# Hand-ordered slices of a decoder trunk: chunks that add first, activations one row tile per piece, their sample part on GpSimd, later x transposes and tables

## The chip, the cores and the metric

The kernel runs on one core of one Trainium2 chip. The metric is the device time of one execution in microseconds (us), as the median of several runs. A core has a matrix engine (TensorE, PE in the profile, with its weight loads as PEld), three engines for elementwise work (VectorE or DVE, ScalarE or ACT, GpSimd or POOL), and queues through which transfers (DMA) are issued; here SyncE (SP) issues the loads of weights and GpSimd the smaller transfers. Each engine works through its own list of instructions in order, and waits at an instruction until what it needs is there.

## The reference, cut to what matters

One layer of a trunk is computed for 256 prompt tokens and for 8 sequences of 8 sample tokens, 320 columns together, in float32. A conditioning vector per sequence gives six rows of modulation; the first two scale and shift the normed input `h`, which then meets one wide weight matrix `w_in`.

```python
mod = jax.nn.silu(c) @ w_ada + b_ada
sh1, sc1, g1, sh2, sc2, g2 = [m[:, None, :] for m in jnp.split(mod, 6, axis=-1)]
h = _rmsnorm(x, norm1_g) * (1 + sc1) + sh1
p = h @ w_in
sizes = [D_QK, D_QK, D_V, D_V, D_POOL, D_MODEL, D_MODEL]
q, k, v, og, u, ga, gb, alr = jnp.split(p, idx, axis=-1)
...
merged = jax.nn.sigmoid(ga) * y_a + jax.nn.sigmoid(gb) * y_b
x = x + g1 * (merged @ w_o)
...
x = x + g2 * ((jax.nn.silu(gate) * up) @ w_down)
```

The prompt has one conditioning vector, each sample sequence has its own. So the modulation of a tile of `h` is one instruction with per-row scalars for the 256 prompt columns, and two instructions (multiply, add) with broadcast operands for the 64 sample columns.

## The kernel before

Activations lie transposed: 16 row tiles `k` of 128 model channels by 320 tokens. Every float32 product is made of three: weights and activations are split into a high part (`whi`, `hh`: a cast on ScalarE, L152 and L293) and a low part (`wlo`, `hl`: a subtraction on VectorE, L153 and L294), and `mm3` (L166 to L168) adds high by high, high by low and low by high in PSUM.

The first head cannot wait until all of `sh1` and `sc1` are known, since `w_ada` is large. So its products with `w_in` are cut along the contracted dimension into slices of row tiles 0-1, 2-3, 4-7 and 8-15 (`SLICES`). For a slice, each of eleven units of 256 output columns (q, k, u, two each of v, og, ga and gb) is worked in pieces of two row tiles; a piece is 12 matmuls. The first three slices are 11, 11 and 22 pieces, 44 in all, and are written out by hand: inside `manual_schedule` each engine takes the instructions in the order of the code. What follows `manual.close()`, the fourth slice first, is ordered by a scheduler.

A unit's partial sum goes from PSUM to SBUF at the end of each slice (`evac`): in the first slice it is copied, by ScalarE for the first unit of a kind and by VectorE for the second; in later slices VectorE adds it (L347, 128x640). PSUM holds two such partial sums (`pmain`, two buffers), so the third unit waits for the evacuation of the first.

Around the pieces stands a plan. Before piece `p` is multiplied, the weights of piece `p + 3` are split (`cut`). The weights of `w_in` arrive in three buffers `raw`, those of `w_ada` in ten buffers `araw`, both on SP's queue, in order: an issue that waits for a free buffer holds up those behind it. After the pieces in `BURST_AT` comes a burst: 32 products (64 in the first two bursts) of the conditioning with `w_ada` on TensorE (L427). When a group of row tiles has all its bursts, it is closed (`close`): a copy on ScalarE, a transpose on TensorE and three small VectorE instructions give `mod`. Groups are row tiles 2-3, 4-7, 8-11 and 12-15, and they close after the bursts at pieces 6, 18, 30 and 41. `x_tr` transposes `x` for a tile (L130, then a copy, L492), `x_norm` multiplies by the reciprocal norm (on GpSimd, L497) and, from tile 8 on, spills the transposed `x` to DRAM from GpSimd's queue (L499). `x_mod` then modulates and splits the tile:

```python
def x_mod(k):
    affine(xhs[k], 1, 0, k)
    hilo(hh[k], hl[k], xhs[k])
```

`affine` is three VectorE instructions (L298 for the prompt columns, L299 and L300 for the sample columns), `hilo` the cast on ScalarE (L293) and the subtraction on VectorE (L294). All tiles of a group are modulated at once, after its close. `tables` issues four transfers from GpSimd's queue (the gate projection's weights `walr`, the constants `cum`, `cst` and the masks); `cum` is cast by VectorE at L595, `walr` is used by `alr_proj` between the second and third unit of the fourth slice. `spills` issues eight more spills from GpSimd's queue after the last of tile 15 (L631), and one small copy (L632). Each transfer of GpSimd's queue waits until the transfer eight before it has landed.

Of the kernel before, what the change touches and what calls it, by code (L numbers as in the profile page):

```python
# [11 lines left out]
F32 = mybir.dt.float32  # L12
# [3 lines left out]
ALU = mybir.AluOpType  # L16
# [4 lines left out]
P = 128  # L21
TP, NB, LS = 256, 8, 8
TS = NB * LS
T = TP + TS
# [15 lines left out]
BURST_AT = (3, 6, 9, 12, 15, 18, 21, 24, 27, 30, 33, 35, 38, 41)  # L40
# [43 lines left out]
def body(tc, A):  # L84
# [198 lines left out]
    def mods(sec, kt):  # L283
        return mod[:, sec * KT + kt, 1:9].unsqueeze(2).broadcast_to([P, NB, LS])

    def s3(ap):
        return ap.rearrange("p (b t) -> p b t", t=LS)
# [4 lines left out]
    def hilo(hi, lo, x):  # L292
        S.copy(hi, x)  # L293
        V.tensor_sub(lo, x, hi.bitcast(F32))  # L294

    def affine(x, a, b, kt):

        V.tensor_scalar(x[:, 0:TP], x[:, 0:TP], modp(a, kt), modp(b, kt), op0=ALU.mult, op1=ALU.add)  # L298
        V.tensor_tensor(s3(x[:, TP:T]), s3(x[:, TP:T]), mods(a, kt), op=ALU.mult)  # L299
        V.tensor_tensor(s3(x[:, TP:T]), s3(x[:, TP:T]), mods(b, kt), op=ALU.add)  # L300

    xspill = dp.tile([KT, P, T], F32, name="xspill")
    mix = ExitStack()
# [71 lines left out]
    with tc.tile_pool(name="head", bufs=1) as xp:  # L375
# [92 lines left out]
        for i in (0, 2, 1):  # L468
            n = P if i < 2 else TS
# [28 lines left out]
            if k >= 8:  # L498
                spilled[:] = [nc.gpsimd.dma_start(xspill[k], xTs[k]).ins]  # L499

        def x_mod(k):

            affine(xhs[k], 1, 0, k)
            hilo(hh[k], hl[k], xhs[k])

        us = units(0)
        us = [u for u in us if u[0] in "qku"] + [u for u in us if u[0] not in "qku"]
        chunks, pieces, begins = [], [], []
        for k0, k1 in SLICES[:-1]:
            begins.append(len(pieces))  # L510
            for u in us[:3]:
                for k in range(k0, k1, 2):
                    pieces.append((u, k, len(chunks), k - k0, 0, k == k0, k + 2 == k1))
                chunks.append((u[2], k0, k1 - k0, 2 * P))
            for n in range(3, len(us), 2):
                for k in range(k0, k1, 2):
                    for j in range(2):
                        pieces.append((us[n + j], k, len(chunks), 0, 2 * P * j, k == k0, k + 2 == k1))
                    chunks.append((us[n][2], k, 2, 4 * P))
        begins.append(len(pieces))  # L520
        raws, cuts = [], {}

        def fetch():
# [61 lines left out]
        first.burst(2)  # L585
        first.close()
        cut(0)
        x_mod(0)
        x_mod(1)
        cut(1)  # L590
        cut(2)
        load()
# [34 lines left out]
        def spills():  # L627

            with tc.issue_after(spilled[0]):
                for k in spill:  # L630
                    nc.gpsimd.dma_start(xspill[k], xTs[k])  # L631
                nc.gpsimd.dma_start(A["o_ps"][0, :, 0:PB - LS, :], A["state_pool"][0, :, LS:PB, :])  # L632
# [3 lines left out]
        def at(p, *fs):  # L636
            plan.setdefault(p, []).extend(fs)
# [3 lines left out]
        for n, p in enumerate(BURST_AT):  # L641
            a = bursts[n]
            at(p, lambda a=a: a.burst(2))
            at(p + 1, load)
            at(p + 2, load)
            if n + 1 == len(bursts) or bursts[n + 1] is not a:
                at(p + 1, a.close)
                for i in range(a.nb):
                    k = a.b0 + i
                    q = BURST_AT[n - a.nb + 1 + i // 2]  # L650
                    at(q, lambda k=k: (x_tr(k), x_norm(k)))
                    at(p + 1, lambda k=k: x_mod(k))
                if a.b0 == 8:
                    at(p + 1, tables)
        for p in range(len(pieces)):
            cut(p + 3)
            mul(p)
            for f in plan.pop(p, ()):
                f()
        assert not plan or min(plan) >= len(pieces)  # L660
        manual.close()
        spills()
        us = [u for u in us if u[0] in "qku" or u[1] == 0]
        k0, k1 = SLICES[-1]
# [680 lines left out]
```

## Time and profile before

| what | us |
|---|---|
| median of 3 runs | 1965.68 |
| lowest, highest | 1963.19, 1965.73 |
| the profiled execution, its own time | 1965.06 |
| its span | 1963.3 |
| TensorE busy in the span | 1921.2 (98%) |
| VectorE, ScalarE, GpSimd busy | 998.9, 820.1, 209.1 |
| mean granted TensorE clock | 0.993 of full |

Times in the views are us from the start of the span. "Busy" on TensorE counts a matmul from its start to its modelled end, and matmuls overlap; how fast it really goes is read from the starts of successive matmuls. A row of the timeline has the start, the duration, the engine, the line, the operation, the tiles out<-in, the shape, and in brackets how long the engine had been idle and what it waited for. The granted clock (PEclk) is given per stretch, 1.00 being full speed. The hand-ordered slices run from about 28 us to about 157 us of the span.

### The profile page before, as it was taken

The page shows a single profiled execution, that of the slowest core. Times are in us where ns is not written, and L with a number is a line of the kernel's source. Part 1 is how long each engine was busy: PE and PEld are TensorE (multiplying, and loading weights), DVE is VectorE, ACT ScalarE, POOL GpSimd, SP SyncE. Part 2 cuts the span into 40 slices and gives each one's busy share as a digit, 9 for nine tenths or more (in the row PEclk, how much of TensorE's full clock was granted, in tenths as well). Part 3 has the DMA queues.
Part 4 walks back from the last instruction along what each step waited for, and adds up shares of the span by engine and source line. Part 5 has one row for each costly group of instructions (what it writes and reads, how often), then busy time and mean ns, then how long its engine had stood idle before and what let it go on. Part 6 is the DMA issues. An engine that isn't in the chain of part 4 may idle for free.

```text
span 1963.3 us, 35017 instructions
## 1 busy us (share of the span) xinstructions
PE 1921.2 (98%) x13990; PEld 1823.2 (93%) x13990; DVE 998.9 (51%) x1853; ACT 820.1 (42%) x1465; POOL 209.1 (11%) x362
## 2 busy tenths in 40 slices
PE   6999999999999999999999999999999999999998
PEld 5778988988899889988999999999999999999998
DVE  3654655656356535665574444444444444444554
ACT  4323553643336433643454333433333434344444
POOL 1132202221121112110030000000000000000000
PEclk9999999999999999999999999999999999999999
DMA  9995558758865787369936554444445444444443
GB/s 331 335 359 195 175 170 287 253 186 302 282 228 163 276 301 255 126 237 330 336 128 204 187 190 140 151 151 145 156 142 159 150 151 150 149 147 146 142 150 106
DMA packets 298179, 400.95 MB, mean 204 GB/s; under 512 B 13104, under 2 KB 249536, under 8 KB 297688
## 3 DMA queue, kind: packets, MB, share of 16 engines
q1 hardware_dynamic: 270336, 301.05, 47.2%
q0 software_dynamic: 27680, 97.67, 13.5%
q8 instruction: 109, 1.79, 0.4%
q14 instruction: 54, 0.44, 0.1%
HBM read 374.23 MB, written 24.67 MB: 203 GB/s over the span
## 4 chain that ended last, share of the span: by engine, by line
PE 82%; DMA 2%; issue 1%; DVE 1%; ACT 1%; POOL 0%; ACTq 0%; POOLq 0%; DVEq 0%
PE ps L168 25%; PE ps L166 25%; PE ps L167 25%; PE pm L256 3%; DMA o_gs<-S 1%; PE pm L130 1%; PE pm L908 1%; PE pm L929 1%; PE pm L873 1%; DMA araw<-w_ada 0%; PE pm L862 0%; DVE wlo L153 0%; DMA o_gp<-sf 0%; PE psy L166 0%; PE pm L884 0%
## 5 line engine op out<-in xcount | busy, mean ns | idle before, releaser
L153 DVE TENSOR_TENSOR wlo<-raw,whi 128x512 fp32r<-128x512 f32 x941 | 651.3, 695 | 791.1 <-ACT whi L152 779.4
L152 ACT CAST whi<-raw 128x512 fp32r<-128x512 f32 x941 | 580.7, 621 | 922.5 <-PE ps L167 832.7
L166 PE MATMUL ps<-hh,whi 128*128 128x320 f32 x1408 | 445.4, 316 | 11.6 <-DVE mg L347 3.8
L168 PE MATMUL ps<-hh,wlo 128*128 128x320 f32 x1408 | 440.0, 314 | 1.5 <-DVE wlo L153 1.5
L167 PE MATMUL ps<-hl,whi 128*128 128x320 f32 x1408 | 440.4, 313 | 0.6 <-DVE hl L294 0.4
L166 PE MATMUL ps<-h2h,whi 128*128 128x320 f32 x1408 | 434.5, 309 | 0.0
L167 PE MATMUL ps<-h2l,whi 128*128 128x320 f32 x1408 | 434.2, 309 | 0.0
L168 PE MATMUL ps<-h2h,wlo 128*128 128x320 f32 x1408 | 434.1, 309 | 0.0
L166 PEld LDWEIGHTS ps<-hh,whi 128*128 128x128 f32 x1408 | 268.1, 190 | 28.7 <-issue 11.8
L168 PEld LDWEIGHTS ps<-hh,wlo 128*128 128x128 f32 x1408 | 267.1, 190 | 12.2 <-issue 7.4
L167 PEld LDWEIGHTS ps<-hl,whi 128*128 128x128 f32 x1408 | 267.9, 190 | 5.1 <-issue 2.4
L166 PEld LDWEIGHTS ps<-h2h,whi 128*128 128x128 f32 x1408 | 264.4, 188 | 1.6 <-ACT ah L293 1.2
L168 PEld LDWEIGHTS ps<-h2h,wlo 128*128 128x128 f32 x1408 | 264.4, 188 | 0.2 <-DVE wlo L153 0.2
L167 PEld LDWEIGHTS ps<-h2l,whi 128*128 128x128 f32 x1408 | 264.5, 188 | 0.0
L167 PE MATMUL ps<-al,whi 128*128 128x320 f32 (+1 forms) x668 | 206.3, 309 | 0.0
L168 PE MATMUL ps<-ah,wlo 128*128 128x320 f32 (+1 forms) x668 | 205.7, 308 | 0.0
L166 PE MATMUL ps<-ah,whi 128*128 128x320 f32 (+1 forms) x668 | 205.7, 308 | 0.0
L167 PEld LDWEIGHTS ps<-al,whi 128*128 128x128 f32 x668 | 125.2, 187 | 0.1
L168 PEld LDWEIGHTS ps<-ah,wlo 128*128 128x128 f32 x668 | 125.2, 187 | 0.0
L166 PEld LDWEIGHTS ps<-ah,whi 128*128 128x128 f32 x668 | 125.2, 187 | 0.0
L166 PE MATMUL ps<-mh,whi 128*128 128x320 f32 x256 | 79.4, 310 | 0.8 <-DVE mg L1035 0.8
L167 PE MATMUL ps<-ml,whi 128*128 128x320 f32 x256 | 79.4, 310 | 0.0
(327 smaller groups left out, 1644.8 us busy)
## 6 DMA issues: line engine op xcount, KB each, us to landing
raw<-w_gu SPq DMA_DIRECT2D x176, 512.0 KB, 3.5
raw<-w_in SPq DMA_DIRECT2D x173, 512.0 KB, 4.1
araw<-w_ada POOLq DMA_DIRECT2D x54, 1024.0 KB, 8.0
raw<-w_down SPq DMA_DIRECT2D x80, 512.0 KB, 3.4
raw<-w_ada SPq DMA_DIRECT2D x64, 512.0 KB, 9.9
S<-state_gla POOLq DMA_DIRECT2D x16, 1024.0 KB, 8.5
o_gs<-S POOLq DMA_DIRECT2D x16, 1024.0 KB, 5.8
raw<-w_o SPq DMA_DIRECT2D x32, 512.0 KB, 5.8
```

Source lines behind the costliest of these rows:

```text
L130: PE.transpose(out, in_, ident[:k, :k])
L152: S.copy(hi, raw)
L153: V.tensor_sub(lo, raw, hi.bitcast(F32))
L166: PE.matmul(ps, lhsT=whi, rhs=xhi, start=start, stop=False)
L167: PE.matmul(ps, lhsT=whi, rhs=xlo, start=False, stop=False)
L168: last_mm[:] = [PE.matmul(ps, lhsT=wlo, rhs=xhi, start=False, stop=stop).ins]
L256: last_ada[:] = [PE.matmul(ps[32 * j:32 * j + 32, 0:2 * P], lhsT=scT[:, k0 + r, :], rhs=ada_raw[n][:, r, 2 * j * P:(2 * j + 2) * P], start ...
L873: PE.matmul(pt, lhsT=E["kdn"][:, s, d * P:(d + 1) * P], rhs=E["vn"][:, s], start=s == 0, stop=s == 1)
L908: PE.matmul(pt[32 * j:32 * j + 32, :], lhsT=qeP[:, d, 4 * gg + j, :], rhs=E["S0", gg, d][:, j], start=False, stop=d == 0, tile_position=(0 ...
L929: PE.matmul(pt, lhsT=E["kpn"][:, j, d * P:(d + 1) * P], rhs=E["vp"][:, gg], start=True, stop=True)
```

## The change

It does six things, all in the first head's slices.

- In each of the first three slices the units v, og, ga and gb (chunks of 512 columns, two pieces to a chunk of two row tiles) come before q, k and u (chunks of 256 columns).
- The modulation of a tile is cut in two. `x_hi` holds `affine` and the cast, `x_lo` the subtraction. After a close the tiles of the group are taken one per piece: tile `i` of a group that closes at piece `p + 1` has its `x_hi` at `p + 1 + i` and its `x_lo` at `p + 2 + i`.
- From tile 2 on the two sample instructions of `affine` go to GpSimd.
- The transposes, norms and spills of tiles 12 to 15 move from the bursts at pieces 33 and 35 to those at 38 and 41.
- `tables` moves from after the close of tiles 8-11 to the burst at piece 38.
- Entries of the plan beyond the last piece (here those of tiles 13 to 15) are issued after `manual.close()`, where the scheduler orders them.

```diff
-    def affine(x, a, b, kt):
+    def affine(x, a, b, kt, eng):
         V.tensor_scalar(x[:, 0:TP], x[:, 0:TP], modp(a, kt), modp(b, kt), op0=ALU.mult, op1=ALU.add)
-        V.tensor_tensor(s3(x[:, TP:T]), s3(x[:, TP:T]), mods(a, kt), op=ALU.mult)
-        V.tensor_tensor(s3(x[:, TP:T]), s3(x[:, TP:T]), mods(b, kt), op=ALU.add)
+        eng.tensor_tensor(s3(x[:, TP:T]), s3(x[:, TP:T]), mods(a, kt), op=ALU.mult)
+        eng.tensor_tensor(s3(x[:, TP:T]), s3(x[:, TP:T]), mods(b, kt), op=ALU.add)
...
-        def x_mod(k):
-            affine(xhs[k], 1, 0, k)
-            hilo(hh[k], hl[k], xhs[k])
+        def x_hi(k):
+            affine(xhs[k], 1, 0, k, V if k < 2 else G)
+            S.copy(hh[k], xhs[k])
+        def x_lo(k):
+            V.tensor_sub(hl[k], xhs[k], hh[k].bitcast(F32))
...
         for k0, k1 in SLICES[:-1]:
-            begins.append(len(pieces))
-            for u in us[:3]:
-                for k in range(k0, k1, 2):
-                    pieces.append((u, k, len(chunks), k - k0, 0, k == k0, k + 2 == k1))
-                chunks.append((u[2], k0, k1 - k0, 2 * P))
             for n in range(3, len(us), 2):
                 for k in range(k0, k1, 2):
                     for j in range(2):
                         pieces.append((us[n + j], k, len(chunks), 0, 2 * P * j, k == k0, k + 2 == k1))
                     chunks.append((us[n][2], k, 2, 4 * P))
-        begins.append(len(pieces))
+            for u in us[:3]:
+                for k in range(k0, k1, 2):
+                    pieces.append((u, k, len(chunks), k - k0, 0, k == k0, k + 2 == k1))
+                chunks.append((u[2], k0, k1 - k0, 2 * P))
...
-        x_mod(0)
-        x_mod(1)
+        x_hi(0)
+        x_hi(1)
+        x_lo(0)
+        x_lo(1)
...
-                    q = BURST_AT[n - a.nb + 1 + i // 2]
+                    q = BURST_AT[n - a.nb + 1 + i // 2] if k < 12 else BURST_AT[n - 1 + i // 2]
                     at(q, lambda k=k: (x_tr(k), x_norm(k)))
-                    at(p + 1, lambda k=k: x_mod(k))
-                if a.b0 == 8:
-                    at(p + 1, tables)
+                    at(p + 2 + i, lambda k=k: x_lo(k))
+                    at(p + 1 + i, lambda k=k: x_hi(k))
+                if a.b0 == 12:
+                    at(BURST_AT[n - 1], tables)
...
-        assert not plan or min(plan) >= len(pieces)
         manual.close()
+        for p in sorted(plan):
+            for f in plan[p]:
+                f()
         spills()
```

Three places in the order of the instructions. The first is VectorE's list where the second slice ends and tiles 4 to 7 are modulated. Before, the last of the four tiles and what follows it (`xh_785` is tile 7, `mg_121` a half of gb):

```order
L298 TENSOR_SCALAR xh_785<-xh_785,mod 128x256
L299 TENSOR_TENSOR xh_785<-xh_785,mod 128x64
L300 TENSOR_TENSOR xh_785<-xh_785,mod 128x64
L294 TENSOR_TENSOR hl_108<-xh_785,hh_92 128x320
L153 TENSOR_TENSOR wlo_1002<-raw_815,whi_1001 128x512
L347 SCALAR_TENSOR_TENSOR mg_121<-ps_1007,mg_121 128x640
L153 TENSOR_TENSOR wlo_1026<-raw_873,whi_1025 128x512
L347 SCALAR_TENSOR_TENSOR mg_121<-ps_1029,mg_121 128x640
```

Now (`xh_678` is tile 4, `xh_685` tile 5):

```order
L298 TENSOR_SCALAR xh_678<-xh_678,mod 128x256
L153 TENSOR_TENSOR wlo_984<-raw_869,whi_983 128x512
L347 SCALAR_TENSOR_TENSOR k_336<-ps_989,k_336 128x640
L508 TENSOR_TENSOR hl_105<-xh_678,hh_89 128x320
L298 TENSOR_SCALAR xh_685<-xh_685,mod 128x256
L153 TENSOR_TENSOR wlo_1013<-raw_893,whi_1012 128x512
L334 TENSOR_TENSOR u_338<-ps_1016,u_338 128x2x256
```

Sixteen instructions of four tiles stood in a row between two splits of weights; now a tile has two, and a split and an evacuation stand between them. The second place is GpSimd's list around the tables. Before (`xT_1447`, `xT_1456` are tiles 12 and 13):

```order
L622 DMA walr<-w_in 128x16x16
L623 DMA cum<-cf 128x800
L624 DMA cst<-cf 128x67
L625 DMA msk<-ci 128x256
L497 TENSOR_TENSOR xh_1449<-xT_1447,rx 128x320
L499 DMA xspill<-xT_1447 128x320
L497 TENSOR_TENSOR xh_1458<-xT_1456,rx 128x320
```

Now, right behind the spills of tiles 12 and 13 (`xT_1659`, `xT_1668` are tiles 14 and 15, `xh_1574` is tile 12):

```order
L626 DMA walr<-w_in 128x16x16
L627 DMA cum<-cf 128x800
L628 DMA cst<-cf 128x67
L629 DMA msk<-ci 128x256
L497 TENSOR_TENSOR xh_1661<-xT_1659,rx 128x320
L499 DMA xspill<-xT_1659 128x320
L497 TENSOR_TENSOR xh_1670<-xT_1668,rx 128x320
L499 DMA xspill<-xT_1668 128x320
L635 DMA xspill<-mg_122 128x320 x4
L635 DMA xspill<-mg_124 128x320 x4
L636 DMA o_ps<-state_pool 8x7168
L299 TENSOR_TENSOR xh_1574<-xh_1574,mod 128x64
```

The tables stand between tiles 13 and 14 instead of ahead of 12, and the sample instructions of tiles 12 to 15 come after all spills and the small copy. The third place is VectorE's list at the start of the fourth slice, now (left out is one more addition to `mod`):

```order
L599 CAST cumr<-cum 128x800
L153 TENSOR_TENSOR wlo_1775<-raw_1772,whi_1774 128x512
L447 TENSOR_TENSOR mod<-pm_1686,bada 128x36
L449 TENSOR_TENSOR mod<-mod,vec 128x36
...
L298 TENSOR_SCALAR xh_1574<-xh_1574,mod 128x256
L298 TENSOR_SCALAR xh_1661<-xh_1661,mod 128x256
L298 TENSOR_SCALAR xh_1670<-xh_1670,mod 128x256
L334 TENSOR_TENSOR u_338<-ps_1673,u_338 128x2x256
L153 TENSOR_TENSOR wlo_1791<-raw_1772,whi_1790 128x512
L336 TENSOR_TENSOR u_338<-ps_1673,u_338 128x8x8 x2
L153 TENSOR_TENSOR wlo_1811<-raw_1808,whi_1810 128x512
```

The cast of `cum` stood among the third slice's splits before, 38 rows ahead of the last group's first `mod`; now it stands two rows ahead of it. On TensorE the products of q with tiles 12 to 15 now come behind those of k with tiles 8 to 11 (24 matmuls): after `hh_96` (tile 11) stood `hh_97`, now stands

```order
L166 MATMUL ps_1737<-hh_96,whi_1756 128x320
L167 MATMUL ps_1737<-hl_112,whi_1756 128x320
L168 MATMUL ps_1737<-hh_96,wlo_1757 128x320
L166 MATMUL ps_1807<-hh_93,whi_1810 128x320
L167 MATMUL ps_1807<-hl_109,whi_1810 128x320
L168 MATMUL ps_1807<-hh_93,wlo_1811 128x320
```

with `ps_1737` the sum of q, `ps_1807` that of k. Behind the gate projection the order is the same as before on every engine.

More of the change, by code (lines that the diff above doesn't have):

```diff
@@ L499, in x_norm @@
                 spilled[:] = [nc.gpsimd.dma_start(xspill[k], xTs[k]).ins]
-        def x_mod(k):
-            affine(xhs[k], 1, 0, k)
-            hilo(hh[k], hl[k], xhs[k])
+        def x_hi(k):
[3 more added lines that the diff above has]
+            V.tensor_sub(hl[k], xhs[k], hh[k].bitcast(F32))
         us = units(0)
         us = [u for u in us if u[0] in "qku"] + [u for u in us if u[0] not in "qku"]
-        chunks, pieces, begins = [], [], []
+        chunks, pieces = [], []
         for k0, k1 in SLICES[:-1]:
-            begins.append(len(pieces))
-            for u in us[:3]:
-                for k in range(k0, k1, 2):
-                    pieces.append((u, k, len(chunks), k - k0, 0, k == k0, k + 2 == k1))
-                chunks.append((u[2], k0, k1 - k0, 2 * P))
             for n in range(3, len(us), 2):
```

## The prediction

> **What bounds the kernel now.** I read the page's busy times first, then TensorE's waits, then its timeline around each wait.
>
> ```profile
> PE 1921.2 (98%) x13990; PEld 1823.2 (93%) x13990; DVE 998.9 (51%) x1853; ACT 820.1 (42%) x1465; POOL 209.1 (11%) x362
> PE ps L166 <- DVE mg L347: 3.8, 1, 3.8
> PE pm L427 <- DMA raw<-w_ada: 3.8, 5, 1.3
> PE ps L166 <- ACT hh L293: 3.4, 3, 2.4
> PE ps L166 <- ACT q L349: 1.4, 1, 1.4
> PE pm L130 <- ACT adasb L433: 1.1, 2, 0.8
> ```
>
> The matrix engine is busy for 98% of the span, and the change touches none of its work. So all it can move is TensorE's own waiting in the slices, 13.5 us in these rows, and the slow clock behind it. A wait's row has the total, the number, the longest. The largest, 3.8 us, is at the hand-over from the second slice to the third:
>
> ```profile
> 88.27 0.88 PE L130 MATMUL pm<-cst,xn 128*128 128x128 f32 x6
> 92.98 0.60 PE L166 MATMUL ps<-hh,whi 128*128 128x320 f32 x1 [3.84 <-DVE mg L347]
> 93.39 0.47 PE L167 MATMUL ps<-hl,whi 128*128 128x320 f32 x1
> 98.72 0.46 PE L166 MATMUL ps<-hh,whi 128*128 128x320 f32 x1
> 84.13 0.41 DVE L298 TENSOR_SCALAR xh<-xh,mod 128x256 f32<-128x256 f32 x1
> 90.89 0.49 DVE L294 TENSOR_TENSOR hl<-xh,hh 128x320 fp32r<-128x320 f32 x1 [0.58 <-ACT hh L293]
> 91.41 0.69 DVE L153 TENSOR_TENSOR wlo<-raw,whi 128x512 fp32r<-128x512 f32 x1
> 92.02 0.82 DVE L347 SCALAR_TENSOR_TENSOR mg<-ps,mg 128x640 f32<-128x640 f32 x1
> ```
>
> From 84.13 to 91.4 VectorE does nothing but modulate four tiles, idling at each for ScalarE's cast; splits and evacuations stand behind, and TensorE has no free PSUM. After the wait successive matmuls start 0.267 us apart (20 steps from 93.39 to 98.72), against 0.147 at full clock (38 steps between these rows):
>
> ```profile
> 156.23 0.31 PE L166 MATMUL ps<-hh,whi 128*128 128x320 f32 x1
> 161.81 0.31 PE L168 MATMUL ps<-hh,wlo 128*128 128x320 f32 x1
> SPq L144 <- DVE wlo L153: 58.8, 22, 8.9
> 84.00:88.00 4.00, 4.00 (x49) 3.15 (x48) 2.66 (x10) 0.92 (x2) 0.00 (x0) 1.00 1.06 374
> 88.00:92.00 4.00, 1.15 (x14) 0.64 (x6) 2.74 (x9) 2.06 (x5) 0.00 (x0) 1.00 0.63 228
> 92.00:96.00 4.00, 3.02 (x11) 3.05 (x12) 3.23 (x5) 1.06 (x3) 2.82 (x4) 0.53 0.70 212
> 128.00:132.00 4.00, 3.42 (x28) 2.45 (x30) 3.19 (x5) 3.09 (x7) 2.12 (x3) 1.00 0.41 119
> ```
>
> The same block holds up the loads: SP waited up to 8.9 us for a split to free a weight buffer, with loads of w_ada queued behind. The last four rows end in clock, DMA share and GB/s: 374 GB/s, then 228 and 212 behind the modulation of tiles 4-7, and 119 behind that of tiles 8-11.
>
> **The change, part by part.**
>
> *Tiles one per piece.* At the second slice's end VectorE now has, per piece of 12 x 0.147 = 1.76 us, a split 0.69, an evacuation 0.82, and 0.41 + 0.49 of modulation: 2.4 us. That is more than a piece, but the sample part has left, five such pieces contain a burst and transposes, and no evacuation falls in the third slice's first two pieces. So the wait of 3.84 goes and with it 20 x 0.12 = 2.4 of slow clock: **6.2 us**. The wait at tiles 8 to 11 (next row) gives **0.4**.
>
> ```profile
> 128.93 0.41 PE L166 MATMUL ps<-hh,whi 128*128 128x320 f32 x1 [0.41 <-ACT whi L152]
> L299 DVE TENSOR_TENSOR xh<-xh,mod 128x64 f32<-128x64 f32 x11 | 2.4, 218 | 0.0
> L497 POOL TENSOR_TENSOR xh<-xT,rx 128x320 f32<-128x320 f32 x8 | 7.2, 898 | 58.1 <-ACT xT L492 58.0
> 92.35 0.86 POOL L497 TENSOR_TENSOR xh<-xT,rx 128x320 f32<-128x320 f32 x1 [23.62 <-ACT xT L492]
> 92.75 1.00 DVE L153 TENSOR_TENSOR wlo<-raw,whi 128x512 fp32r<-128x512 f32 x1
> ```
>
> *Sample part on GpSimd.* The trace has no 128x64 product there. Its cost lies between VectorE's 0.22 and GpSimd's 0.90 for five times the columns; I take 0.3. Tile 7's two stand behind two norms and two spills of tiles 8 and 9, which come with the burst just before the third slice, so tile 7 arrives late there: **-0.5** (0 to -1). All others have pieces to spare, except tiles 12 to 15, below. In the last two rows a split that overlaps a GpSimd product takes 1.00 instead of 0.69. By the Trainium skill (SBUF — State Buffer, Who interferes with whom) a VectorE instruction with two SBUF inputs and a GpSimd instruction that reads SBUF lock each other out for a whole instruction. This pair agrees in kind. By the rule the 28 products moved could hold VectorE for 28 x 0.3 = 8 us, an estimate; VectorE has that to spare between hand-overs, so the sum would lose about 1 us at most.
>
> *First pieces.* Both `x_lo` now stand behind both tiles' `affine`, which holds the second matmul by about 0.25; the first chunk is 512 KB instead of 256. Together **-0.4** (0 to -0.9).
>
> *Chunk order.*
>
> ```profile
> 36.44 0.41 PE L166 MATMUL ps<-hh,whi 128*128 128x320 f32 x1 [1.42 <-ACT q L349]
> 35.16 0.62 ACT L152 CAST whi<-raw 128x512 fp32r<-128x512 f32 x1 [3.74 <-DMA raw<-w_in]
> ```
>
> The fourth chunk was needed by the fourth piece, and ScalarE waited 3.74 us for it with q's evacuation behind. Three 512-KB chunks now cover six pieces before a fourth is needed: **+1.4**.
>
> *Loads of w_ada.* In the stretch from 28 to 153 the bursts idled 2.8 us for them:
>
> ```profile
> L427 PE MATMUL pm<-raw,scT 128*32 128x256 f32 (+1 forms) x512 | 28.5, 356 | 2.8 <-DMA raw<-w_ada 2.8
> ```
>
> TensorE comes to the last bursts 6.2 + 0.4 + 1.4 - 0.9 = 7.1 us sooner. The loads do too: against 374 GB/s the three low rows above lost 4 us x (146 + 162 + 255) / 374 = 6.0 us of transfer, and the eight late spills of 160 KB (1.3 MB, 3.4 us) now come behind the last burst. I take **+2.5** (0 to 2.8).
>
> *Entry of the fourth slice.* Before:
>
> ```profile
> 155.70 0.40 PE L166 MATMUL ps<-hh,whi 128*128 128x320 f32 x1
> 176.45 0.31 PE L607 MATMUL pm<-hh,wal 128*128 128x320 f32 x1
> 107.00 1.19 POOL L622 DMA_DIRECT2D walr<-w_in  x1
> L499 POOL DMA_DIRECT2D xspill<-xT x8 | 4.7, 587 | 0.0
> cum<-cf POOLq DMA_DIRECT2D x1, 400.0 KB, 8.8
> 117.30 0.57 DVE L595 CAST cumr<-cum 128x800 fp32r<-128x800 f32 x1
> 124.01 1.93 PE L427 MATMUL pm<-raw,scT 128*32 128x256 f32 x32
> ```
>
> 108 matmuls (15.9 us at full clock) took 20.75; with adasb's wait of 0.8 the loss is 5.7 us. Now a new wait stands there: VectorE's cast of `cum` is ahead of the last `mod`, of u's evacuation and of the low parts for k. From the end of the burst at piece 38, GpSimd does two norms, two spill issues and walr's (0.7 for transpose and copy, then 0.9 + 0.6 + 0.9 + 0.6 + 1.2), so `cum` is issued at +4.9 and lands 8.8 later by its row, at +13.7. The last burst ends at +8.1 (transposes 0.9, three pieces 5.3, burst 1.9). So `cum` lands 5.6 after it; I take X = 5, since the w_ada loads have ended by then. The nearest bound below, half that flight, is X = 1. VectorE then needs the cast 0.57, split 0.69, `mod` 0.57, three L298 1.23, u's 0.69 and 0.35, a split 0.69: k's PSUM is free at X + 4.8. TensorE wants it after transposes 0.9, 48 matmuls 7.05 and the close 0.3, at 8.25: stall X - 3.45 = 1.55, and 0.4 more for k's first low part. The last cast ahead of `hh` of tile 12 (0.62) waits for a buffer that k's matmuls free, then come `hh` 0.46 and `hl` 0.49: 1.75. GpSimd's late sample part has by then had some 14 us and lies beside this. Together 3.7 idle, and slow clock after it, 13 x 0.12 = 1.6: 5.3 against 5.7, **+0.4**. With X = 1 it is 1.75 (+4.0); with X = 5.6 and two slow stretches 7.5 (-1.8).
>
> ```profile
> 240.64 0.41 PE L166 MATMUL ps<-hh,whi 128*128 128x320 f32 x1 [1.29 <-ACT whi L152]
> 242.31 0.59 PE L168 MATMUL ps<-hh,wlo 128*128 128x320 f32 x1 [0.82 <-DVE wlo L153]
> 240.00:244.00 4.00, 2.54 (x10) 2.28 (x11) 3.38 (x4) 2.88 (x6) 1.55 (x1) 0.80 0.00 0
> ```
>
> That short idling slows the clock is read here: two waits of 2.1 us together, and the granted clock is 0.80. By the Trainium skill (TensorE: Matmul & The Clock Gate, Part 1) the clock falls after an idle window of about 3.4 us; by that the entry would cost 3.7 instead of 5.3, and the sum would gain 1.6. This row differs, and I keep to the row.
>
> **Sum:** 6.2 + 0.4 - 0.5 - 0.4 + 1.4 + 2.5 + 0.4 = 10.0 us. Behind the gate projection the order is unchanged, so the block only shifts. Against the profiled execution's 1965.06 that is 1955.1; the median of the runs shown is 0.6 above that execution: **1955.5**. All terms at their low ends give 6.2 + 0.4 - 1 - 0.9 + 1.4 + 0 - 1.8 = 4.3 (1961.4), at their high ends 14.8 (1950.9).
>
> **Rivals.**
>
> (a) *The loads become the bound.* For: DMA shares at the ceiling in most stretches, and 2.8 us of waits already. Against: the 6.0 us recovered. If the loads come only 3.6 us sooner where TensorE comes 7.1, 3.5 us of burst waits are added and the 2.5 is lost: gain 4, 1961.5.
>
> (b) *Everything hidden.* `cum` lands early (8.8 us was under full load), and the entry costs 1.75: gain 14 to 15, 1951.
>
> (c) *Slower: VectorE stuck at the cast of `cum`.* Place: the entry; price: one us per us of X beyond 3.45. For: `walr`, small pieces, is ahead in the queue. Against: 8.4 to 8.8 us was measured with the load at its ceiling. The 9.6 us of the other terms are eaten when X - 3.45 + 5.35 - 5.7 = 9.6, at X = 13.4, a landing twice as slow; at X = 20 the time is 1972.
>
> (d) *The hand-over stays.* GpSimd's list holds tile 7, or 2.4 us of VectorE work per piece does not fit, and half of the 6.2 returns: 1959.
>
> **Chances.** Forecast 0.58 (own range 1952 to 1958.5), (a) 0.14, (b) 0.12, (c) 0.04, (d) 0.12. The range 1950.5 to 1961.5 takes in the low and high ends. A difference of 0.2%, 3.9 us, is what a measurement of this kernel can tell: the forecast, (b), (d) and half of (a) are faster by more, 0.87 with a little kept back; same 0.09; slower 0.04.
>
> **What would show it.** No wait near 89 and a granted clock of 1.00 there; no wait for q near 36; DMA near 375 GB/s through 88 to 132; bursts idling under 1 us; VectorE idle before the cast of `cum` with DMA as releaser, and TensorE waiting for u's evacuation right after; the fourth slice entered some 9 us sooner. A gain below 4 us, or waits of several us at new places among the pieces, would make this wrong.

## The result, and the profile after

| | before | changed |
|---|---|---|
| median of 6 runs each, us | 1963.19 | 1951.28 |
| lowest to highest | 1962.89 to 1965.73 | 1948.69 to 1956.34 |
| ratio, 95% interval | | 0.994, 0.9928 to 0.9951 |
| profiled execution: its own time, span | 1965.06, 1963.3 | 1948.69, 1946.9 |

The change saves 11.9 us by the medians; 10.0 had been forecast. (The kernel before came out 2.5 us lower here than the median of three runs that the forecast started from.) The profiled execution of the changed kernel is its fastest and that of the kernel before one of its slower ones, so 16.4 us lie between the two traces. In its view of TensorE's waits these rows bear on the slices (total, number, longest; the longest of the first row stands ahead of the first slice, as before):

```profile
PE ps L166 <- ACT hh L504: 3.6, 3, 2.4
PE ps L167 <- DVE hl L508: 3.6, 4, 1.2
PE pm L427 <- DMA raw<-w_ada: 2.3, 3, 1.1
```

The 2.3 us for `w_ada` all lie before 28 us, ahead of the slices. The wait of 3.8 us for `mg` and q's 1.4 are gone, but 3.6 us of waits for `hl` have come. In TensorE's timeline they stand just where the one large wait stood (start, duration, instruction, idle time before it and what ended it):

```profile
89.22 0.42 PE L167 MATMUL ps<-hl,whi 128*128 128x320 f32 x1 [1.06 <-DVE hl L508]
93.17 0.42 PE L167 MATMUL ps<-hl,whi 128*128 128x320 f32 x1 [1.05 <-DVE hl L508]
94.52 0.41 PE L166 MATMUL ps<-hh,whi 128*128 128x320 f32 x1 [0.34 <-ACT hh L504]
96.17 0.42 PE L167 MATMUL ps<-hl,whi 128*128 128x320 f32 x1 [1.24 <-DVE hl L508]
```

These are tile 5, tile 6, and tile 7 twice: 3.7 us in sum, where one wait of 3.84 was. The windows of the same stretch (their last three columns are granted clock, DMA share and GB/s) show what did get better:

```profile
88.00:92.00 4.00, 2.94 (x20) 2.64 (x18) 2.21 (x7) 1.63 (x4) 1.54 (x3) 1.00 0.99 362
92.00:96.00 4.00, 1.54 (x7) 0.93 (x6) 2.42 (x4) 1.50 (x3) 1.88 (x4) 1.00 0.91 273
96.00:100.00 4.00, 3.83 (x46) 2.71 (x47) 1.54 (x3) 0.40 (x2) 0.00 (x0) 1.00 1.05 407
128.00:132.00 4.00, 4.00 (x30) 4.00 (x29) 3.66 (x6) 1.60 (x3) 0.00 (x0) 1.00 1.03 369
```

The clock stayed at 1.00 (0.53 before), and the loads ran at 362, 273 and, later, 369 GB/s where they had 228, 212 and 119. The products with `w_ada` from 28 us to the last burst's end no longer wait for their loads; this group had 2.8 us of idle time before:

```profile
L427 PE MATMUL pm<-raw,scT 128*32 128x256 f32 (+1 forms) x512 | 27.1, 355 | 0.0
```

Where the time came from is read most safely as the distances between marks that both traces have: the first matmul of the first slice, the starts of the bursts by piece, and the first matmul of the gate projection.

| stretch | before | changed | gain | forecast |
|---|---|---|---|---|
| start to burst 3 (chunk order, first pieces) | 11.72 | 9.55 | 2.2 | 1.0 |
| burst 3 to 21 | 46.25 | 46.25 | 0 | 0 |
| burst 21 to 24 (hand-over to tiles 4-7) | 14.75 | 12.73 | 2.0 | 5.7 |
| burst 24 to 35 (tiles 8-11) | 30.17 | 28.50 | 1.0 + 0.6 moved | 0.4 |
| burst 35 to the end of burst 41 (w_ada) | 21.46 | 17.23 | 4.2 | 2.5 |
| end of burst 41 to the gate projection | 23.66 | 20.84 | 3.4 - 0.6 moved | 0.4 |
| sum | 148.01 | 135.10 | 12.9 | 10.0 |

"Moved" are the transposes of two tiles, 0.6 us, which left one stretch for the other. The total was nearly right, and its parts were not: the hand-over gave a third of its term, and four others gave more. Each column is one execution: a second one of the changed kernel needed 136.15 in all, with 1.6 us more just behind burst 24, where its clock fell. The remaining 3.6 us between the traces lie behind the slices, where the work is unchanged; the section on the hardware returns to them.

### The profile page after: what moved, and what is told of

Same layout as the page of the kernel before. It is cut to its first block, busy times and chain, and to the rows that moved or that the text cites. A ratio compares the mean times of both kernels' runs of the same rounds, so it can differ in the third digit from the quotient of the medians.

```text
span 1946.9 us, 35031 instructions
## 1 busy us (share of the span) xinstructions
PE 1910.8 (98%) x13990; PEld 1815.3 (93%) x13990; DVE 993.8 (51%) x1825; ACT 819.8 (42%) x1465; POOL 217.4 (11%) x390
## 4 chain that ended last, share of the span: by engine, by line
PE 86%; DVE 1%; ACT 1%; issue 0%; ACTq 0%; DVEq 0%
PE ps L168 26%; PE ps L166 26%; PE ps L167 26%; PE pm L256 3%; PE pm L130 1%; PE pm L936 1%; PE pm L915 1%; PE pm L880 1%; PE pm L869 0%; PE pm L810 0%; DVE wlo L153 0%; PE pm L891 0%; PE psy L166 0%; PE pm L871 0%; PE psy L167 0%
## 5 line engine op out<-in xcount | busy, mean ns | idle before, releaser
L1253 POOL CAST ax<-ah 128x128 fp32r<-128x128 f32 x11 | 10.4, 947 | 619.6 <-ACT ah L293 619.6
```

The lines of the kernel that those rows point to most:

```text
L1253: G.tensor_copy(tx[:, :, 0:TS], th[:, :, TP:T].bitcast(F32))
```

## The experiments

The theory was the prediction's: the hand-over's gain comes from spreading the tiles, and what is left of its waits is tile 7 behind GpSimd's norms and spills. The rival: a tile per piece is simply late, whichever engine does the sample part. Unless a run is said to be timed in rounds, it is one execution beside one of the kernel before on the same chip (1962.64 us for the first four; 1963.33 for the next three and for the pairs with later norms; for the run without spread, 1962.85 as the median of nine). "The stretch" is burst 21 to 24.

**Sample part back on VectorE.**

```diff
-            affine(xhs[k], 1, 0, k, V if k < 2 else G)
+            affine(xhs[k], 1, 0, k, V)
```

> The changed kernel with the sample part of every tile back on VectorE. In the changed kernel TensorE waits 3.7 us in four pieces between 88 and 97 us (1.06 for tile 5, 1.05 for tile 6, 0.34 + 1.24 for tile 7). Theory A (GpSimd: its norms of tiles 8 and 9 lock VectorE's subtraction of tile 6, and tile 7's sample part stands behind them and two spills): tile 7's 1.6 goes, tile 6's lock may stay, so about 2.1 us of waiting there, and the burst at piece 24 starts 1 to 2 us sooner than 97.1. Rival B (one tile per piece is simply too late, because ScalarE's cast and VectorE's steps wait for each other in turn): 3.5 us or more, wherever the sample part runs.

TensorE's waits in the timeline of this kernel, and two of its windows:

```profile
90.27 0.41 PE L167 MATMUL ps<-hl,whi 128*128 128x320 f32 x1 [1.65 <-DVE hl L508]
94.67 0.41 PE L167 MATMUL ps<-hl,whi 128*128 128x320 f32 x1 [1.49 <-DVE hl L508]
95.94 0.41 PE L166 MATMUL ps<-hh,whi 128*128 128x320 f32 x1 [0.27 <-ACT hh L504]
97.58 0.41 PE L167 MATMUL ps<-hl,whi 128*128 128x320 f32 x1 [1.24 <-DVE hl L508]
96.00:100.00 4.00, 2.76 (x26) 1.69 (x30) 2.52 (x4) 0.92 (x2) 0.00 (x0) 0.86 1.00 373
100.00:104.00 4.00, 4.00 (x35) 2.76 (x28) 0.06 (x1) 1.27 (x3) 0.85 (x2) 0.71 1.05 394
```

4.65 us of waits, more than the rival's 3.5, and a slow clock after them; 1956.66 us in all, 4.4 to 5.4 above the changed kernel's two medians (1952.27 below, 1951.28 above). So GpSimd's list is not what makes the tiles late as a whole: without its two instructions per tile they are later. The slices are 4.8 us longer: 0.9 in the stretch, 1.6 of slow clock behind it, 1.3 at the fourth slice with a wait of 1.45 us for u's evacuation, and 1.0 elsewhere. The 1.6 may be chance, since an unedited execution showed the same fall. So the part costed as a loss of 0.5 us is a gain of some 3 to 5.

**The norms and spills of tiles 8 to 11 one burst later.**

```diff
-q = BURST_AT[n - a.nb + 1 + i // 2] if k < 12 else ...
+q = BURST_AT[n - a.nb + 1 + i // 2 + (a.b0 == 8)] if k < 12 else ...
```

> The changed kernel with the transposes, norms and spills of tiles 8 to 11 one burst later (after pieces 24 and 27 instead of 21 and 24), so that nothing of tiles 8 and 9 is in GpSimd's list between tiles 4 and 7. Theory A: only tile 5's wait is left, about 1.1 us, and the subtraction of tile 6 takes 0.49 again instead of 1.27. Rival B: the waits stay at 3.7 us. Both: the span falls by what the waits fall, since no wait for w_ada follows (there is none after 28 us in the changed kernel).

TensorE's waits of the stretch in this kernel:

```profile
89.11 0.41 PE L167 MATMUL ps<-hl,whi 128*128 128x320 f32 x1 [1.68 <-DVE hl L508]
94.16 0.41 PE L167 MATMUL ps<-hl,whi 128*128 128x320 f32 x1 [1.24 <-DVE hl L508]
```

Two waits are left of four, together 2.9 us: between the two expectations. Tile 6's 1.05 is gone, and its `hl` takes 0.48 us again. Of tile 7's two waits the 0.34 is gone, but the 1.24 stays to the hundredth. Tile 5's grew from 1.06 to 1.68, as the transposes that stood ahead of it on TensorE, 0.6 us, came a burst later. So the norms and spills cost about 1.4 us, most of it at tile 6; what was predicted, tile 7 behind them, is 0.34 of it. 1950.43 us.

**Tiles 4 to 7 two per piece.**

```diff
+j = i // 2 if a.b0 == 4 else i
-at(p + 2 + i, lambda k=k: x_lo(k))
-at(p + 1 + i, lambda k=k: x_hi(k))
+at(p + 2 + j, lambda k=k: x_lo(k))
+at(p + 1 + j, lambda k=k: x_hi(k))
```

> The changed kernel with tiles 4 to 7 modulated two per piece instead of one, so that the last of them is done two pieces sooner and ahead of the norms of tiles 8 and 9. Theories A and B both expect at most 0.5 us of waiting between 80 and 100 us, a burst at piece 24 at about 93.5 instead of 97.1, and a span 3 to 3.7 us shorter. If instead TensorE waits for PSUM there (for an evacuation behind two tiles' steps, as in the kernel before), about 2 us or more come back and the spreading by single tiles was needed.

The only wait of that stretch in the timeline of this kernel:

```profile
90.54 0.38 PE L166 MATMUL ps<-hh,whi 128*128 128x320 f32 x1 [1.46 <-DVE u L336]
```

All waits for tiles are gone, and one for PSUM is left: 1.46 us, between the two expectations. The stretch is 9.67 us, 3.1 less than the changed kernel's. So it was the spread that made tiles 5 to 7 late. Bursts 35 and 38 then took 0.6 and 1.1 us more, with a wait of 0.46 us for `w_ada`: TensorE now comes to them about as early as the loads allow. Of the 3.1 us only 1.3 are left at the gate projection, where 3 to 3.7 had been expected of the span. 1950.97 us.

**The chunk order alone, in the kernel before.**

```diff
 for k0, k1 in SLICES[:-1]:
-    (q, k, u, then the wide chunks)
+    (the wide chunks, then q, k, u)
```

> The kernel before with only the order of the chunks changed (v, og, ga, gb before q, k, u in the first three slices). Theory: the wait for q near 36 us (1.42) is gone and the burst at piece 3 starts 2 us sooner than 40.16; the hand-over near 89 keeps a wait of 3.8 us or more, and the waits for w_ada in the last bursts stay or grow, since the loads are still held up by the modulations: 0 to 2 us less than before in all. Rival: the w_ada waits were due to the chunks' order, and go with it: 4 to 6 us less.

Two rows of TensorE's timeline and a window, of this kernel:

```profile
91.47 0.39 PE L166 MATMUL ps<-hh,whi 128*128 128x320 f32 x1 [3.84 <-DVE k L347]
127.27 0.61 PE L166 MATMUL ps<-hh,whi 128*128 128x320 f32 x1 [3.21 <-DVE mg L347]
92.00:96.00 4.00, 4.00 (x20) 4.00 (x19) 2.49 (x6) 0.62 (x1) 1.66 (x3) 0.60 0.96 295
```

The wait for q is gone (10.43 us to burst 3, from 11.72). The hand-over's 3.84 us stays to the hundredth, for k in place of `mg`, and the one at tiles 8-11 grows from 0.41 to 3.21. The bursts' waits for `w_ada` behind 28 us are gone, which the theory did not expect; the 4 to 6 us of the rival did not come with it, since TensorE now waits earlier. 1962.14 us: by itself this part is worth 0.5 us, no difference that can be told. The opposite, all but the chunk order, wasn't tried: with q, k and u first, the second piece of the third slice needs tiles 6 and 7, which a tile per piece has not made by then.

**The late places undone** (x transposes of tiles 12-15 back at the bursts of pieces 33 and 35, the tables back at piece 31).

```diff
-q = BURST_AT[n - a.nb + 1 + i // 2] if k < 12 else BURST_AT[n - 1 + i // 2]
+q = BURST_AT[n - a.nb + 1 + i // 2]
-if a.b0 == 12:
-    at(BURST_AT[n - 1], tables)
+if a.b0 == 8:
+    at(p + 1, tables)
```

> The changed kernel with the x transposes of tiles 12 to 15 back at the two bursts of pieces 33 and 35 and the tables back at piece 31. Theory A (the late places do what I charged to them: the spills, the tables and x pieces no longer stand among the loads of w_ada): TensorE waits for raw<-w_ada again at the bursts of pieces 38 and 41, 1 to 3 us in sum, and the two bursts, which took 1.9 us each in the changed kernel, lengthen by that. Rival B (the chunk order took those waits away, since the kernel before with only its chunk order changed no longer showed them): no wait for w_ada after 30 us, both bursts 1.9 us long, and the first adaLN-row matmul comes within 1 us of the changed kernel's 163.7 us.

From the timelines of VectorE, GpSimd and TensorE of this kernel:

```profile
127.18 1.70 DVE L153 TENSOR_TENSOR wlo<-raw,whi 128x512 fp32r<-128x512 f32 x1
127.40 0.88 POOL L497 TENSOR_TENSOR xh<-xT,rx 128x320 f32<-128x320 f32 x1
134.11 0.39 PE L166 MATMUL ps<-hh,whi 128*128 128x320 f32 x1 [1.13 <-DVE mg L347]
147.43 1.06 PE L427 MATMUL pm<-raw,scT 128*32 128x256 f32 x12 [2.26 <-DMA raw<-w_ada]
```

Theory A: the wait for `w_ada` is back, 2.26 us, and the last burst takes 5.1 us instead of 1.9. Beside it VectorE's split takes 1.70 instead of 0.69 while a norm runs on GpSimd, and an evacuation comes 1.13 late. 1954.22 us, 2 to 3 above the changed kernel.

**Only the tables early** (the second half of that edit).

> The changed kernel with only the tables back at piece 31. Theory A (VectorE stuck 3.17 us at the cast of cum is what TensorE pays for at the entry of the fourth slice): VectorE's idle time there goes, and TensorE's waits at 151 and 156 us, 1.7 us in sum, fall below 0.7 us. Rival B (those waits come from tiles 12 to 15 being cast and subtracted in turn by ScalarE and VectorE after the last piece, whatever VectorE did before): VectorE's idle time goes and TensorE's waits stay at 1.3 us or more; a wait for w_ada of up to 1 us may come back, since the tables' loads stand among those of w_ada again.

In this kernel `cum` is cast at 126.16, far from the last `mod`; VectorE idles there 2.52 us for ScalarE's cast instead of 3.17 for `cum`. TensorE's timeline at tile 12:

```profile
156.66 0.56 PE L166 MATMUL ps<-hh,whi 128*128 128x320 f32 x2 [0.92 <-ACT hh L504]
157.43 0.41 PE L167 MATMUL ps<-hl,whi 128*128 128x320 f32 x1 [0.21 <-DVE hl L508]
```

They are the changed kernel's 0.92 and 0.22 again, as rival B had it for tile 12. Their sum, 1.1 us, lies between the two bounds: the two small stalls for k, 0.5 us in sum, are gone, and burst 38 took 0.55 us more: 1951.40 us, no difference. The place of the tables is worth nothing that one execution can tell, so what the last edit measured belongs to the transposes and spills.

**GpSimd's part alone, in the kernel before** (sample part of tiles 2 to 15 on GpSimd, all else old).

```diff
-            affine(xhs[k], 1, 0, k)
+            affine(xhs[k], 1, 0, k, V if k < 2 else G)
```

> The kernel before with one part alone: the sample part of the modulation of tiles 2 to 15 on GpSimd, with the old chunk order, all tiles of a slice at one piece and the old places. Theory A (unloading VectorE is what helps: eight VectorE operations less per slice at the hand-over): TensorE's wait of 3.84 us at the third slice falls to 1 to 2.5 us and the one at the fourth slice with it; the time is 2 to 5 us below the kernel before. Rival B (VectorE still casts and subtracts all four tiles in one lump, and GpSimd's two operations per tile and the lock with VectorE's subtraction add to it): the wait at the third slice stays at 3 us or grows, and the time is within 2 us of the kernel before or above it.

The hand-over in this kernel, TensorE's timeline and three windows:

```profile
92.85 0.39 PE L166 MATMUL ps<-hh,whi 128*128 128x320 f32 x1 [2.51 <-DVE mg L347]
88.00:92.00 4.00, 2.33 (x37) 1.29 (x26) 2.81 (x7) 2.19 (x6) 0.11 (x1) 1.00 0.82 294
92.00:96.00 4.00, 3.15 (x21) 3.18 (x22) 3.62 (x5) 1.55 (x4) 2.83 (x4) 1.00 0.78 221
96.00:100.00 4.00, 4.00 (x49) 3.04 (x47) 1.55 (x3) 0.62 (x1) 0.00 (x0) 1.00 1.01 366
```

3.84 became 2.51 (2.5 to the tenth, the edge of what theory A gave), and the clock stayed at 1.00: the stretch is 10.71 us against 14.75, of which 2.4 are the slow clock that did not come. From the end of burst 41 to the gate projection it took 19.89 us against 23.66: of the kernel before's three waits for tiles at the fourth slice (0.36, 0.26 and 0.74) the last two are gone, and the slow clock behind them. 1958.81 us, 4.5 below the kernel before: the larger of the two parts that were run alone. Behind 28 us the bursts kept 3.7 us of waits for `w_ada`.

**No spread at all** (the changed kernel, tiles 4-7 all modulated at one piece and subtracted at the next: `j = 0` in the edit of the pairs).

> The changed kernel with tiles 4 to 7 not spread at all: all four modulated and cast at the first piece after the burst and all four subtracted at the next, the sample part on GpSimd. Two parts alone have already given: GpSimd's part under the old order cut the stretch from the burst of piece 21 to that of piece 24 from 14.75 to 10.71 us, and one tile per piece with the sample part on VectorE left it at 13.67 us. Theory A (of the two, GpSimd's part is the gain and the spread costs: with one tile per piece, tiles 5, 6 and 7 come just after their first matmul is due): TensorE's waits in the stretch fall from 3.7 us to 2.7 us or less in one place, for a PSUM buffer, and the stretch from 12.73 us to 11.5 us or less. Rival B (the lump delays the evacuations of k and u as before the change, and the spread is what the new chunk order needs): a wait of 3.5 us or more for an evacuation, the stretch 12.5 us or longer, with a clock below 1.00 after the wait.

TensorE's one wait and the window after it, of this kernel:

```profile
91.42 0.39 PE L166 MATMUL ps<-hh,whi 128*128 128x320 f32 x1 [2.75 <-DVE u L336]
92.00:96.00 4.00, 4.00 (x20) 4.00 (x19) 1.16 (x2) 0.62 (x1) 0.00 (x0) 0.62 0.91 303
```

The wait is 0.05 us above theory A's bound, and 1 us less than the spread's 3.7. But it is one wait, the clock fell after it to 0.62, and the stretch is 13.10 us, rival B's. 1952.09 us. So neither held as put: the spread splits the idle time into pieces and makes more of it, and in these two executions the clock made up the difference. The whole time is the changed kernel's.

**Looking for a better version.** Pairs with the later norms, a gap between the pairs (`j = 2 * (i // 2)`), and, timed in five rounds on one chip, the pairs, the gap and the changed kernel again:

> The changed kernel with tiles 4 to 7 two per piece and the x transposes and spills of tiles 8 to 11 one burst later, the two edits that each took about half of what was left at the third slice. If the two causes are separate (tiles late by the spread; VectorE and GpSimd in each other's way at the norms): the waits between 88 and 98 us fall from 3.7 us to 1.5 us (u's evacuation alone, which the paired tiles showed) or less, the burst of piece 24 begins at 93.5 to 94.3 us, and the first adaLN-row matmul 1.5 to 3 us sooner than in the changed kernel. If they are one cause, it is no better than the paired tiles alone: waits of 1.5 us and the first adaLN-row matmul at 162 to 162.5 us.

> A candidate: tiles 4 and 5 modulated and cast at the first piece after the burst and subtracted at the second, tiles 6 and 7 at the third and fourth, so that no cast of a tile stands on ScalarE ahead of the weight cast whose low part VectorE does just before u's evacuation. If u's evacuation was late by those casts (the 1.46 us wait of the paired tiles), the waits from 88 to 98 us are 0.5 us or less and the burst of piece 24 begins 2.5 to 4 us sooner than in the changed kernel counted from the burst of piece 21 (8.7 to 10.2 us instead of 12.73); the time is 1.5 to 4 us below the changed kernel's. If the evacuation itself is what TensorE waits for, the wait stays at 1 to 1.5 us, and the time is that of the paired tiles, 0 to 1.5 us below the changed kernel's.

> The kernel with tiles 4 to 7 two per piece once more, timed in five rounds. Its first adaLN-row matmul came 1.4 us sooner than in the changed kernel; if nothing later gives that back, its time is 0.5 to 2 us below the changed kernel's; if the clock of TensorE after 220 us and the loads decide, the two are within 1 us.

> The changed kernel unedited, in the same five rounds as the two candidates, to compare with them: 1949 to 1954 us, and 10 to 13 us below the kernel before.

Pairs with later norms waited 2.08 us for u's evacuation, more than either expectation, and took 1950.09 us. With the gap that wait went, and one of 1.91 for tile 6's `hl` took its place, with a clock of 0.74 after it; here too neither expectation held. In five rounds:

| kernel | median us | lowest to highest | ratio to before, 95% |
|---|---|---|---|
| changed, again | 1952.27 | 1949.78 to 1956.27 | 0.9947, 0.9935 to 0.9960 |
| tiles 4-7 in pairs | 1949.63 | 1948.96 to 1951.75 | 0.9931, 0.9917 to 0.9944 |
| pairs with a gap | 1950.96 | 1949.97 to 1952.70 | 0.9939, 0.9927 to 0.9952 |

The kernel before took 1962.85 us in the same rounds. The pairs' median is 2.6 us below the changed kernel's, more than the 0.5 to 2 that were expected; the intervals overlap, so this is likely and not shown.

## Why the prediction was right, and where it was not

*The hand-over* is the step that failed. It said that with a tile per piece "the wait of 3.84 goes", and that all tiles but the seventh "have pieces to spare". Measured: 3.7 us of waits are left, and the stretch gave 2.0 us of the 5.7 charged to it. VectorE's, GpSimd's and ScalarE's timelines of the changed kernel show why:

```profile
88.68 0.48 DVE L508 TENSOR_TENSOR hl<-xh,hh 128x320 fp32r<-128x320 f32 x1
91.24 0.69 DVE L153 TENSOR_TENSOR wlo<-raw,whi 128x512 fp32r<-128x512 f32 x1 [1.75 <-ACT whi L152]
91.84 1.27 DVE L508 TENSOR_TENSOR hl<-xh,hh 128x320 fp32r<-128x320 f32 x1
91.89 0.87 POOL L497 TENSOR_TENSOR xh<-xT,rx 128x320 f32<-128x320 f32 x1
93.30 0.31 POOL L299 TENSOR_TENSOR xh<-xh,mod 128x64 f32<-128x64 f32 x1
93.68 0.29 POOL L300 TENSOR_TENSOR xh<-xh,mod 128x64 f32<-128x64 f32 x1
94.01 0.46 ACT L504 CAST hh<-xh 128x320 fp32r<-128x320 f32 x1 [2.81 <-POOL xh L300]
```

The working added up VectorE's busy time per piece, compared it with the piece of 1.76 us, and took the excess for hidden. What it missed is the order between engines. ScalarE takes the tile's cast and then the weights' (`hh`, then `whi`); VectorE takes the weights' low part, then the tile's, and then the next tile's modulation (`wlo`, `hl`, L298), on which the next `hh` waits. So for each tile the two engines run one after the other. Later in the same kernel, between tiles 10 and 11, where neither an evacuation nor a norm interferes, one round reads:

```profile
123.84 0.41 DVE L298 TENSOR_SCALAR xh<-xh,mod 128x256 f32<-128x256 f32 x1
124.70 0.61 ACT L152 CAST whi<-raw 128x512 fp32r<-128x512 f32 x1
125.35 0.69 DVE L153 TENSOR_TENSOR wlo<-raw,whi 128x512 fp32r<-128x512 f32 x1 [1.10 <-ACT whi L152]
126.36 0.41 DVE L298 TENSOR_SCALAR xh<-xh,mod 128x256 f32<-128x256 f32 x1
```

A round takes 2.52 us, though VectorE is busy for only 1.6 of them; with an evacuation in it, tile 9 to 10, it takes 3.24. There nothing is due at once, so TensorE does not wait. At the hand-over VectorE idles 1.75 us in the round of tile 6, since ScalarE also copies two transposed tiles (L492) between `hh` and `whi`. And the `hl` of tiles 5 and 7 are placed directly ahead of the piece that uses them (after pieces 21 and 23, for 22 and 24), that of tile 6 one piece ahead: tiles 4 and 6 had one spare piece, 5 and 7 none. Tile 7 does come behind two norms and two spills of GpSimd, and its two products take 0.31 and 0.29 (0.3 was estimated). Tile 6's `hl` takes 1.27 instead of 0.49 beside a GpSimd norm; with later norms it took 0.48, and tile 6's wait was gone. By the Trainium skill (SBUF — State Buffer, Who interferes with whom) a VectorE instruction with two SBUF inputs and a GpSimd instruction that reads SBUF shut each other out; the trace agrees, at 0.8 us on the path.

The 2.0 us that did come are, by the rows, the slow clock's 2.4 less what TensorE loses around four waits instead of one, since the waits are as long as before. That the clock held is luck: in one of four executions with these four waits it fell behind them and took 1.6 us back. The spread and the move to GpSimd came in one change; the runs part their shares: GpSimd's part alone cuts the wait from 3.84 to 2.51 (old order) or 2.75 (new order, no spread); the spread then raises it to 3.7, and pairs lower it to 1.46. The gain belonged to the part that was charged as a loss. Tile 7 behind GpSimd's norms, the reason given for that loss of 0.5, is 0.34. Rival (d), "the hand-over stays", was right about this place and wrong about the time, since other terms made up for it.

*Loads of w_ada* gave 4.2 for 2.5, above the bound of 2.8: the bursts of pieces 38 and 41 had been longer than a burst without waits by 2.3 and 1.9 us, and I had sized them by the idle time in a row, which counts less than a burst loses around its waits. The mechanism held: the waits came back, 2.26 us, in the run that put the transposes, spills and tables back. The chunk order alone also showed none, but there TensorE was late itself, by the 3.21 us at tiles 8-11. How much of the 4.2 is due to the later spills and how much to loads that VectorE no longer holds up was not separated. Rival (a), loads as the bound, did not come in the changed kernel; the paired version, 1.4 us ahead of it by the gate projection, shows first waits of 0.2 to 0.5 us.

*Entry of the fourth slice.* The mechanism came as described, place by place; its sizes were too high. From the changed kernel's timelines, the cast on VectorE, then tile 12 on TensorE, and the transfer's row:

```profile
146.64 0.58 DVE L599 CAST cumr<-cum 128x800 fp32r<-128x800 f32 x1 [3.17 <-DMA cum<-cf]
156.06 0.56 PE L166 MATMUL ps<-hh,whi 128*128 128x320 f32 x2 [0.92 <-ACT hh L504]
156.83 0.41 PE L167 MATMUL ps<-hl,whi 128*128 128x320 f32 x1 [0.22 <-DVE hl L508]
cum<-cf POOLq DMA_DIRECT2D x1, 400.0 KB, 6.7
```

`cum` landed 6.7 us after its issue instead of 8.8, at X = 146.64 - 142.84 = 3.8 after the last burst, not 5. By the prediction's own formula k's stall is then X - 3.45 = 0.35; the trace has 0.29. Tile 12 cost 1.66 with its ramps (1.75 forecast), the low part 0.23 (0.4), and the clock did not fall (1.6). Some 2.3 us instead of 5.3. The other side of this term, the loss of the kernel before, shrank with GpSimd's part alone too: in the old order that took 3.8 us off this stretch, a gain that the prediction did not count for it. Rival (b), in which `cum` lands early and all is hidden, named 1951 and so has the time; of its reasons the entry is as shown, while at the hand-over nothing was hidden. Rival (c) did not come: X was far from 13.4. With the tables early the 0.5 us of k's part vanish and nothing else changes, so tile 12's wait is its own.

*Chunk order and first pieces* gave 2.2 for 1.0. The order alone gave 1.3; executions whose code is the same up to burst 3 needed 8.9 to 9.8 us to there, so the rest is partly scatter. *Tiles 8-11* gave 1.0 for 0.4. Of the 13.5 us that the prediction called waiting in the slices, 3.8 stood ahead of the first slice, out of the change's reach; no term was drawn from them. The sum was near because the errors had both signs: -3.7 at the hand-over, +1.2, +0.6, +1.7 and +3.0 elsewhere. That they nearly cancelled is luck. The measured median, 4.2 us below the forecast, lies below the forecast's own range (1952 to 1958.5) and near the low end of the whole one; 2.5 of the 4.2 are the kernel before, which measured lower. Of the signs that were named, the clock of 1.00 near 89, q, the bursts, the wait for `cum` and the fourth slice's start, 9.4 us sooner, came; "no wait near 89" and loads near 375 GB/s throughout (273 at 92 to 96) did not.

## What to carry to other kernels

When work is spread over pieces, compare each part's finish with its first use along the whole alternation of engines, not one engine's busy time with the piece. Price two edits at one place separately; a part that only moves 2 x 0.2 us per tile to an idle engine may carry the gain, because it shortens a chain that all four tiles repeat. Where idle time of a few us can slow the matrix engine's clock, but need not, time in rounds and profile twice: one execution may show a gain or a loss of 1 to 2 us that is the clock's alone.

## What the runs showed of the hardware

The clock did not follow the length of the wait. After 2.51 us in one piece it stayed at 1.00; after 1.91 it fell to 0.74. After the 1.46 us of the paired tiles it stayed at 1.00; with the sample part on VectorE it fell to 0.62 after 1.45 us at the fourth slice:

```profile
156.69 0.39 PE L166 MATMUL ps<-hh,whi 128*128 128x320 f32 x1 [1.45 <-DVE u L336]
156.00:160.00 4.00, 3.31 (x13) 3.34 (x14) 2.54 (x9) 0.56 (x2) 0.00 (x0) 0.62 0.76 235
```

The changed kernel's four waits left it at 1.00 in the first execution, as they did in the two kernels with the late places or the tables undone; in the execution that was profiled in the five rounds, with the same waits to 0.02 us, the windows after them read:

```profile
96.00:100.00 4.00, 3.45 (x33) 2.12 (x37) 1.92 (x4) 0.00 (x0) 0.00 (x0) 0.73 1.05 405
100.00:104.00 4.00, 4.00 (x30) 3.25 (x23) 1.04 (x2) 1.71 (x4) 1.87 (x3) 0.84 1.05 388
```

This cost 1.6 us (burst 24 to 27: 9.59 instead of 7.96). The same holds behind the slices, where every kernel has waits of 1.29 and 0.82 us shortly ahead of the first product with `cumr`, as here in the changed kernel, whose window has a clock of 1.00 where the kernel before had 0.80:

```profile
227.87 0.41 PE L166 MATMUL ps<-hh,whi 128*128 128x320 f32 x1 [1.29 <-ACT whi L152]
229.54 0.41 PE L168 MATMUL ps<-hh,wlo 128*128 128x320 f32 x1 [0.82 <-DVE wlo L153]
228.00:232.00 4.00, 3.18 (x21) 2.92 (x22) 4.00 (x5) 3.23 (x6) 0.94 (x1) 1.00 0.00 0
```

From the gate projection to the first product with `cumr`, seven of the fourteen profiled executions took 67.7 to 67.8 us at full clock, and seven 68.5 to 69.5 us with a fall; the kernel before is among the latter, with 69.2. Both executions of the unedited changed kernel kept the clock, and both of the paired one had the fall, so that an edit has some part in it can't be ruled out; with equal waits in all of them I read it as mostly chance. These 0.8 to 1.7 us are part of the 3.6 us by which the two first traces differ behind the slices. By the Trainium skill (TensorE: Matmul & The Clock Gate, Part 1) the clock falls after an idle window of about 3.4 us that runs free of the program. That equal waits end both ways agrees with a window that runs free; the falls after 1.91 us, and after 1.29 and 0.82 with work between, came sooner than that figure.
